# Storing the outputs of a mixture of experts: 8 KB runs for experts 0 to 5, own buffers and transfers for experts 6 and 7, three semaphores by turns on one DMA queue

## The chip, the cores and the metric

The kernel runs on one core of one Trainium2 chip. The metric is device time in microseconds (us) of one execution. A profile of one execution gives a span, from the first to the last instruction, and what each engine did in it. The engines are PE (TensorE, matmuls), DVE (VectorE), ACT (ScalarE), POOL (GpSimd) and SP (SyncE). Transfers between device memory (HBM) and the on-chip memory (SBUF) are carried out by 16 DMA engines. A transfer is issued by an engine's queue: here most come from Pool's queue (the profile calls it software_dynamic), two from SyncE's (hardware_dynamic). Each transfer counts a semaphore up by 16 when its data has landed.

## The reference

Eight experts, each a two-layer network with a ReLU between, over 256 tokens of width 512. Data is fp32 outside; the kernel computes in bf16 with fp32 sums.

```python
n_experts, capacity, hidden, expert_hidden = 8, 256, 512, 2048
# x [8, 256, 512], w1 [8, 512, 2048], w2 [8, 2048, 512], all float32

def reference(x, w1, w2):
    h = np.matmul(x, w1)
    h = np.maximum(h, 0)
    return np.matmul(h, w2).astype(np.float32)   # [8, 256, 512]
```

Each expert has 4 MB of w1 and 4 MB of w2 in fp32, so 64 MB of weights are read in all. x and the output are 4 MB each.

## The kernel before

P is 128 (partitions), E, C, H, F are 8, 256, 512, 2048, and MC = C/P = 2. R = E\*C/P = 16 is the number of rows of x in one partition. The views say which row of a DRAM tensor goes to which partition. In the output's view, partition p of an expert holds rows 2p and 2p+1, that is 4 KB in a row in DRAM:

```python
    x_v = x.rearrange("e (pp r) k -> (e pp) (r k)", r=R)
    w1_v = w1.rearrange("e (p ko) n -> p e (ko n)", ko=K1)
    w2_v = w2.rearrange("e (p h j) n -> p e h (j n)", h=2, j=JH)
    out_v = out.rearrange("e (p mo) k -> p e (mo k)", mo=MC)
    # ...
    out_sb = allot("out_sb", [P, E, MC, H], FP32)
```

Weights are converted to bf16 on the way in, by Pool's queue, into four slots each for w1 and w2. The order of the loads, and a semaphore for each slot:

```python
    d_w = {
        (w, i): sem(f"d_w{w}_{i}")
        for w, slots in [(1, (0, 2, 3)), (2, (0, 1, 2, 3))]
        for i in slots
    }
    d_half, d_pool, d_last = sem("d_half"), sem("d_pool"), sem("d_last")
    # ...
    loads = []                                   # (which weight, experts, half, halves)
    for es in [(0, 1), (2, 3)]:
        loads += [(1, es, 0, 2), (2, es, 0, 2)]
    loads += [(1, (4, 5), 0, 2), (2, (4,), 0, 2), (2, (5,), 0, 2)]
    for e in range(6, E - 1):
        loads += [(1, (e,), 0, 2), (2, (e,), 0, 2)]
    loads += [(1, (E - 1,), 0, 2), (2, (E - 1,), 0, 1), (2, (E - 1,), 1, 1)]
```

SyncE loads the first quarter of x (`x_head`), tells TensorE of every load that has landed, and at the end stores the last expert's output:

```python
        sp = nc.sync
        for i, (w, es, h, n) in enumerate(loads):
            sp.wait_ge(*landed[i])
            sp.sem_inc((c_w1, c_w2)[w - 1], n * len(es) if w == 2 else len(es))
        sp.wait_ge(v_last, MC)
        sp.dma_start(
            out_v[:, E - 1, :], out_sb[:, E - 1].rearrange("p m h -> p (m h)")
        ).then_inc(d_last, 16)
```

Pool issues the rest of x, then the loads (each waits only until its slot is free), one tiny store of 16 x 16 values between the two halves of the last w2, and, once that tiny store has landed, one store of the outputs of experts 0 to 6:

```python
        pool = nc.gpsimd
        pool.dma_start(x_sb[:, HEAD * H:], x_v[:, HEAD * H:]).then_inc(d_pool, 16)
        # ... identity ...
        for i, (w, es, h, n) in enumerate(loads):
            old = es[-1] - NS
            if w == 2 and 2 in es:
                tc.wait_critical_data_deps()
                pool.wait_ge(*after_transposes(K1 * MC))
            if old >= 0 and h == 0:
                if w == 1:
                    pool.wait_ge(*after_hidden(old, NG))
                else:
                    pool.wait_ge(*after_outputs(old, MC))
            if i == len(loads) - 1:
                pool.wait_ge(s_event, 3)
                pool.dma_start(
                    out_v[:16, 0, :16], out_sb[:16, 0, 0, :16]
                ).then_inc(d_pool, 16)
            # ... src, dst of the load ...
            pool.dma_start(dst, src).then_inc(landed[i][0], 16)
        pool.wait_ge(s_event, 4)
        pool.wait_ge(d_pool, 32)
        pool.dma_start(
            out_v[:, :E - 1, :], out_sb[:, :E - 1].rearrange("p e m h -> p e (m h)")
        ).then_inc(d_pool, 16)
```

x is transposed by TensorE through PSUM (`xt_ps`); DVE and ACT copy it into `xT`, in the order of rows in which the outputs then come out. DVE takes the outputs out of PSUM (`o_ps`, two banks of 128 x 512), but for the last half, which ACT takes:

```python
        def copy_xt(copy, ko, m):
            return copy(
                xT[:, ko, m].rearrange("k (ep r2) -> k ep r2", r2=R // MC),
                xt_ps[m][:].rearrange("k r2 ep -> k ep r2"),
            )
        # ...
        for e in range(E):
            for m in range(MC):
                if e == E - 1 and m == 1:
                    break
                dve.wait_ge(*after_outputs(e, m + 1))
                cp = dve.tensor_copy(out_sb[:, e, m, :], o_ps[m][:])
                cp.then_inc(v_last if e == E - 1 else c_o)
            if e in (4, E - 2):
                dve.drain().then_inc(s_event)
        # ... on ACT, after the last expert's last matmul:
        act.copy(out_sb[:, E - 1, 1, :], o_ps[1][:]).then_inc(v_last)
```

TensorE takes each expert in two halves of the hidden layer and then the output layer (16 pairs of matmuls into the two banks). At the end of each half it takes one count of `c_o`, which stands for a bank of outputs that has been copied out:

```python
        def half():
            # ... 32 matmuls into h_ps ...
                if ends:
                    take(c_h, 1)
                    if i == n - 1:
                        take(c_o, MC // 2)
        def expert():
            take(c_w1, 1)
            loop("half", reg["half"], 2, half)
            for k in range(K2):
                if k % JH == 0:
                    take(c_w2, 1)
                # ... 2 matmuls into o_ps, the last pair counts s_pe ...
```

Of the kernel before, what the change touches and what calls it, by code (L numbers as in the profile page):

```python
# [8 lines left out]
FP32 = mybir.dt.float32  # L9
# [7 lines left out]
def kernel(  # L17
# [8 lines left out]
    P = 128  # L26
    E, C, H = x.shape
    F = w1.shape[2]
    MC = C // P
# [3 lines left out]
    R = E * C // P  # L33

    HEAD = 4

    NS = 4
# [8 lines left out]

    x_v = x.rearrange("e (pp r) k -> (e pp) (r k)", r=R)
    w1_v = w1.rearrange("e (p ko) n -> p e (ko n)", ko=K1)  # L50
    w2_v = w2.rearrange("e (p h j) n -> p e h (j n)", h=2, j=JH)
    out_v = out.rearrange("e (p mo) k -> p e (mo k)", mo=MC)


    places, free = {}, FIRST_FREE
# [1 line left out]
    def allot(name, shape, dtype):  # L57
        nonlocal free
        places[name] = free
        t = nc.alloc_sbuf_tensor_at(name, shape, dtype, offset=free)  # L60
        free += math.prod(shape[1:]) * mybir.dt.size(dtype)
        return t


    out_sb = allot("out_sb", [P, E, MC, H], FP32)
    w1_sb = allot("w1_sb", [P, NS, K1 * F], BF16)
    w2_sb = allot("w2_sb", [P, NS, K2 * H], BF16)
    xT = allot("xT", [P, K1, MC, E * P], BF16)
# [4 lines left out]
    x_sb = w2_sb[:, 2, :]  # L73
    X_AT = W2_AT + 2 * K2 * H * 2

    xt_ps = [nc.alloc_psum_tensor(f"xt_ps{i}", [P, R // MC, P], BF16) for i in range(MC)]
    h_ps = [nc.alloc_psum_tensor(f"h_ps{i}", [P, GJ * C], FP32) for i in range(UG)]
    o_ps = [nc.alloc_psum_tensor(f"o_ps{i}", [P, H], FP32) for i in range(MC)]

    def sem(name):  # L80
        return tc.alloc_semaphore(name)

    d_w = {
        (w, i): sem(f"d_w{w}_{i}")
        for w, slots in [(1, (0, 2, 3)), (2, (0, 1, 2, 3))]
        for i in slots
    }
    d_half, d_pool, d_last = sem("d_half"), sem("d_pool"), sem("d_last")  # L90


    s_event = sem("s_event")
    s_pe, v_last = sem("s_pe"), sem("v_last")

    def after_transposes(n):
        return s_pe, n

    def after_hidden(e, groups):
        return s_pe, K1 * MC + e * (NG + MC) + groups  # L100

    def after_outputs(e, halves):
        return s_pe, K1 * MC + e * (NG + MC) + NG + halves
# [10 lines left out]
    loads = []  # L114
# [3 lines left out]
    for e in range(6, E - 1):  # L118
        loads += [(1, (e,), 0, 2), (2, (e,), 0, 2)]
    loads += [(1, (E - 1,), 0, 2), (2, (E - 1,), 0, 1), (2, (E - 1,), 1, 1)]  # L120
    landed, counts = [], {}
    for w, es, h, _ in loads:
        s = d_half if h else d_w[w, es[0] % NS]
        counts[id(s)] = counts.get(id(s), 0) + 16
        landed.append((s, counts[id(s)]))

# [4 lines left out]
    with tc.tile_critical(no_gpsimd_drain=True):  # L133

        sp = nc.sync
        for i, (w, es, h, n) in enumerate(loads):
            sp.wait_ge(*landed[i])
            sp.sem_inc((c_w1, c_w2)[w - 1], n * len(es) if w == 2 else len(es))
        sp.wait_ge(v_last, MC)
        sp.dma_start(  # L140
            out_v[:, E - 1, :], out_sb[:, E - 1].rearrange("p m h -> p (m h)")
        ).then_inc(d_last, 16)


        pool = nc.gpsimd
        pool.dma_start(x_sb[:, HEAD * H:], x_v[:, HEAD * H:]).then_inc(d_pool, 16)  # L146
        pool.memset(identity[:], 0.0).then_inc(s_event)  # L147
        pool.wait_ge(s_event, 1)

# [1 line left out]
            out=identity[:],  # L151
# [7 lines left out]
# [13 lines that stand above are left out]


                pool.wait_ge(s_event, 3)
                pool.dma_start(  # L175
                    out_v[:16, 0, :16], out_sb[:16, 0, 0, :16]
                ).then_inc(d_pool, 16)
            e, ne, at_slot = es[0], len(es), es[0] % NS
            if w == 2:
                src = w2_v[:, e:e + ne, h:h + n, :].rearrange("p e h n -> p e (h n)")  # L180
                dst = w2_sb[:, at_slot:at_slot + ne, h * JH * H:(h + n) * JH * H]
            else:
                src, dst = w1_v[:, e:e + ne, :], w1_sb[:, at_slot:at_slot + ne, :]
            pool.dma_start(dst, src).then_inc(landed[i][0], 16)  # L184
        pool.wait_ge(s_event, 4)
        pool.wait_ge(d_pool, 32)
        pool.dma_start(  # L187
            out_v[:, :E - 1, :], out_sb[:, :E - 1].rearrange("p e m h -> p e (m h)")
        ).then_inc(d_pool, 16)

        def copy_xt(copy, ko, m):
            return copy(  # L194
                xT[:, ko, m].rearrange("k (ep r2) -> k ep r2", r2=R // MC),
                xt_ps[m][:].rearrange("k r2 ep -> k ep r2"),
            )


        dve = nc.vector  # L200
        dve.sem_inc(c_xt[0], 1)
        for ko in range(K1):
            dve.wait_ge(*after_transposes(ko * MC + 1))
            copy_xt(dve.tensor_copy, ko, 0).then_inc(c_xt[0])
        dve.sem_inc(c_o, MC)
        for e in range(E):
            for m in range(MC):
                if e == E - 1 and m == 1:
                    break
                dve.wait_ge(*after_outputs(e, m + 1))  # L210
                cp = dve.tensor_copy(out_sb[:, e, m, :], o_ps[m][:])  # L211
                cp.then_inc(v_last if e == E - 1 else c_o)
            if e in (4, E - 2):
                dve.drain().then_inc(s_event)  # L214


        act = nc.scalar
        act.sem_inc(c_xt[1], 1)
        for ko in range(K1):
            act.wait_ge(*after_transposes(ko * MC + 2))  # L220
            copy_xt(act.copy, ko, 1).then_inc(c_xt[1])
# [6 lines left out]
                    mybir.ActivationFunctionType.Relu,  # L228
                ).then_inc(c_h)
        act.wait_ge(*after_outputs(E - 1, MC))  # L230
        act.copy(out_sb[:, E - 1, 1, :], o_ps[1][:]).then_inc(v_last)  # L231

# [1 line left out]
        pe = nc.tensor  # L236
# [45 lines left out]
        def last_column(step):  # L282

            return (P - 1) * step * 2
# [25 lines left out]
                t.then_inc(s_pe)  # L310

        pe.wait_ge(s_event, 2)
        pe.wait_ge(d_pool, 16)
        x_first = X_AT + last_column(K1)
        pe.reg_mov(reg["x"], x_first)
        loop("transposes", reg["x"], x_first + K1 * 2, transposes)
# [116 lines left out]


        pool.drain()
        pool.wait_ge(d_pool, 48).then_inc(s_event)
        pool.wait_ge(d_last, 16).then_inc(s_event)


# [28 lines left out]
```

## Time and profile before

| | |
|---|---|
| device time, median of 3 runs | 180.59 us (180.55 to 180.62) |
| span of the profiled execution | 178.7 us |
| TensorE busy | 127.7 us, 71% of the span |
| DVE busy | 15.8 us, 9% |
| ACT busy | 38.7 us, 22% |
| POOL busy | 10.2 us, 6% |
| HBM read and written | 71.30 MB and 4.20 MB |
| one eviction, DVE, 128 x 512 fp32 | 687 ns |
| one copy of transposed x, DVE and ACT, 128 x 1024 | 1225 ns and 1012 ns |

The page cuts the span into 40 equal slices (4.47 us each) and gives for each the busy share in tenths; the row "DMA" is the mean busy share of the 16 DMA engines, "GB/s" what they moved. A weight load reads fp32 and writes bf16, and GB/s counts it about once, by what lands. Further parts list the DMA queues with their packets, the chain of work that ended last, and for each transfer the time from issue to landing. L264 is the line of the helper that records every matmul, L138 is SyncE's wait for a load, L211 and L231 are the evictions on DVE and ACT.

### The profile page before, as it was taken

To read this page: it belongs to the slowest core of one execution; us is meant where nothing else is said; L and a number is where in the kernel's file an instruction comes from. 1 tells how busy PE (TensorE), PEld (TensorE's weight loads), DVE (VectorE), ACT (ScalarE), POOL (GpSimd) and SP (SyncE) were. 2 spreads that over 40 slices of the span, in tenths; PEclk is the share of its full clock that TensorE was granted. 3 is DMA by queue.
4 is the path that set the end of the run, shared out by engine and by line. 5 is a ranking of instruction groups with operands and counts; after the bars stand their busy time and mean duration, and the time that the engine had idled before them with its cause. 6 is when DMAs were issued, how large, how long until landed. Compare 5 with 4: busy or idle time off the path is not lost. (4 is left out here: it accounts for less than half of the span.)

```text
span 178.7 us, 2096 instructions
## 1 busy us (share of the span) xinstructions
PE 127.7 (71%) x832; PEld 89.8 (50%) x832; DVE 15.8 (9%) x20; ACT 38.7 (22%) x38; POOL 10.2 (6%) x21
## 2 busy tenths in 40 slices
PE   0008610792049999993079999999999999769990
PEld 0006600691014695693024984884794695359630
DVE  0204320000000200200000200200200200200010
ACT  0202420062000062044000260251152062004400
POOL 6100010000000002101000110100200000002000
PEclk9999999999657999999759999999999999978999
DMA  6999998998999999999899899999999989989996
GB/s 211 244 220 205 235 227 183 235 231 183 231 235 205 205 235 209 202 235 231 180 235 231 191 224 235 205 205 235 209 202 235 231 180 235 231 182 220 327 424 259
DMA packets 3744, 40.37 MB, mean 226 GB/s; under 512 B 288, under 2 KB 288, under 8 KB 1312
## 3 DMA queue, kind: packets, MB, share of 16 engines
q0 software_dynamic: 3456, 38.80, 97.3%
q1 hardware_dynamic: 288, 1.57, 2.4%
HBM read 71.30 MB, written 4.20 MB: 422 GB/s over the span
## 5 line engine op out<-in xcount | busy, mean ns | idle before, releaser
L264 PE MATMUL o_ps<-w_sb,hT 128*128 x256 | 60.3, 396 | 18.9 <-PEq L239 18.8
L264 PE MATMUL h_ps<-xT,w_sb 128*128 x512 | 61.4, 282 | 11.8 <-PEq L239 11.8
L264 PEld LDWEIGHTS h_ps<-xT,w_sb 128*128 x512 | 58.0, 146 | 16.1 <-issue 12.5
L225 ACT ACTIVATE hT<-h_ps 128x1024 bf16<-128x1024 f32 x32 | 32.7, 1023 | 111.2 <-PE h_ps L264 111.2
L264 PEld LDWEIGHTS o_ps<-w_sb,hT 128*128 128x128 bf16 x256 | 25.3, 101 | 51.2 <-issue 24.6
L211 DVE COPY out_sb<-o_ps 128x512 f32<-128x512 f32 x15 | 9.7, 687 | 141.2 <-PE o_ps L264 141.2
L264 PE MATMUL xt_ps<-identity,w_sb 128*128 128x128 bf16 x64 | 7.6, 312 | 15.5 <-PEq L239 15.5
L264 PEld LDWEIGHTS xt_ps<-identity,w_sb 128*128 x64 | 6.5, 147 | 16.3 <-issue 16.3
L184 POOL DMA_DIRECT2D w_sb<-in_w_dram x12 | 7.4, 618 | 104.3 <-PE h_ps L264 57.3
L194 ACT COPY xT<-xt_ps 128x1024 bf16<-128x1024 bf16 x4 | 4.0, 1012 | 11.8 <-PE xt_ps L264 11.8
L194 DVE COPY xT<-xt_ps 128x1024 bf16<-128x1024 bf16 x4 | 4.9, 1225 | 11.8 <-PE xt_ps L264 11.8
L187 POOL DMA_DIRECT2D out_dram<-out_sb x1 | 1.0, 962 | 34.0 <-DMA out_dram<-out_sb 34.0
L194 ACT ACT_TABLE_LOAD x1 | 1.3, 1283 | 7.0 <-DVE w_sb L132 7.0
L231 ACT COPY out_sb<-o_ps 128x512 f32<-128x512 f32 x1 | 0.6, 585 | 5.9 <-PE o_ps L264 5.9
L132 DVE CAST w_sb<-x_head 128x2048 bf16<-128x2048 f32 x1 | 1.2, 1227 | 5.5 <-DMA x_head<-in_x_dram 5.5
L175 POOL DMA_DIRECT2D out_dram<-out_sb x1 | 0.5, 509 | 14.7 <-DVEq L214 14.7
L146 POOL DMA_DIRECT2D w_sb<-in_x_dram x1 | 0.7, 679 | 0.8 <-POOLq L452 0.8
L150 POOL TENSOR_SCALAR_AFFINE_SELECT identity<-identity 128x128 bf16<-128x128 bf16 x1 | 0.3, 283 | 0.2 <-POOL identity L147 0.2
L147 POOL MEMSET identity<- 128x128 bf16 x1 | 0.2, 223 | 0.0
L452 POOL MEMSET const-float32-0.0<- 128x1 f32 x1 | 0.1, 93 | 0.2 <-issue 0.2
L452 POOL MEMSET const-bfloat16-1.0<- 128x1 bf16 x1 | 0.1, 95 | 0.0
L452 POOL MEMSET const-uint8-127<- 128x1 uint8 x1 | 0.1, 95 | 0.0
(1 smaller groups left out, 0.1 us busy)
## 6 DMA issues: line engine op xcount, KB each, us to landing
w_sb<-in_w_dram POOLq DMA_DIRECT2D x5, 4096.0 KB, 47.9
w_sb<-in_w_dram POOLq DMA_DIRECT2D x5, 2048.0 KB, 51.5
out_dram<-out_sb POOLq DMA_DIRECT2D x1, 3584.0 KB, 12.9
w_sb<-in_w_dram POOLq DMA_DIRECT2D x2, 1024.0 KB, 44.1
w_sb<-in_x_dram POOLq DMA_DIRECT2D x1, 1536.0 KB, 11.5
x_head<-in_x_dram SPq DMA_DIRECT2D x1, 1024.0 KB, 4.7
out_dram<-out_sb SPq DMA_DIRECT2D x1, 512.0 KB, 3.1
out_dram<-out_sb POOLq DMA_DIRECT2D x1, 1.0 KB, 34.4
```

Source lines behind the costliest of these rows:

```text
L132: nc.vector.tensor_copy(x_sb[:, :HEAD * H], x_head[:])
L146: pool.dma_start(x_sb[:, HEAD * H:], x_v[:, HEAD * H:]).then_inc(d_pool, 16)
L150: pool.affine_select(out=identity[:], in_=identity[:], compare_op=mybir.AluOpType.not_equal, fill=1.0, base=0, pattern=[[-1, P]], channel_ ...
L175: pool.dma_start(out_v[:16, 0, :16], out_sb[:16, 0, 0, :16]).then_inc(d_pool, 16)
L184: pool.dma_start(dst, src).then_inc(landed[i][0], 16)
L187: pool.dma_start(out_v[:, :E - 1, :], out_sb[:, :E - 1].rearrange("p e m h -> p e (m h)")).then_inc(d_pool, 16)
L194: return copy(xT[:, ko, m].rearrange("k (ep r2) -> k ep r2", r2=R // MC), xt_ps[m][:].rearrange("k r2 ep -> k ep r2"),)
L211: cp = dve.tensor_copy(out_sb[:, e, m, :], o_ps[m][:])
L225: act.activation(hT[:, g * GJ:(g + 1) * GJ, :].rearrange("p a c -> p (a c)"), h_ps[g % UG][:], mybir.ActivationFunctionType.Relu,).then_in ...
L231: act.copy(out_sb[:, E - 1, 1, :], o_ps[1][:]).then_inc(v_last)
L264: return pe.add_instruction(inst)
L452: nc = _bacc.Bacc("TRN2", target_bir_lowering=False, num_devices=1)
```

## The change

The outputs of experts 0 to 5 are gathered in pairs of experts. Expert 2i lies on partitions 0 to 63 and expert 2i+1 on partitions 64 to 127, four rows to a partition, so that what one partition holds of an expert is 8 KB in a row in DRAM instead of 4 KB. Experts 6 and 7 get a buffer `last_sb` with two rows to a partition on all 128 partitions; there partition 64t + q holds rows 4q + 2t and 4q + 2t + 1. The order of rows in which PSUM receives the outputs is changed to suit, by the copies of x. The store of experts 0 to 6 becomes two: one of experts 0 to 5, one of expert 6. All Pool transfers count three semaphores by turns, and each waits for the one three before it in place of having semaphores by slot. The aim is longer runs in the stores and fewer semaphores.

```diff
-    out_v = out.rearrange("e (p mo) k -> p e (mo k)", mo=MC)
+    HP = P // 2
+    PAIRS = E // 2 - 1
+    out_pairs = out[:2 * PAIRS].rearrange("(i s) (q r) k -> s q i (r k)", s=2, r=2 * MC)
+    out_v = out.rearrange("e (q t m) k -> t q e (m k)", t=2, m=MC)
@@
-    out_sb = allot("out_sb", [P, E, MC, H], FP32)
+    out_sb = allot("out_sb", [P, PAIRS, 2 * MC, H], FP32)
+    last_sb = allot("last_sb", [P, 2, MC, H], FP32)
@@ (the semaphores by slot)
-    d_w = { ... }
-    d_half, d_pool, d_last = sem("d_half"), sem("d_pool"), sem("d_last")
+    d_pool, d_last = [sem(f"d_pool{i}") for i in range(3)], sem("d_last")
@@
+    of_load = [i + 1 for i in range(len(loads) - 1)] + [len(loads) + 1]
+    small, bulk, bulk2 = len(loads), len(loads) + 2, len(loads) + 3
+
+    def landed(i):
+        return d_pool[i % 3], 16 * (i // 3 + 1)
@@ (SyncE)
-            sp.wait_ge(*landed[i])
+            sp.wait_ge(*landed(of_load[i]))
...
         sp.dma_start(
-            out_v[:, E - 1, :], out_sb[:, E - 1].rearrange("p m h -> p (m h)")
+            out_v[:, :, E - 1, :], last_sb[:, 1].rearrange("p m h -> p (m h)")
         ).then_inc(d_last, 16)
@@ (Pool; all its transfers go through queue)
+        def queue(i, dst, src):
+            if i >= 3:
+                pool.wait_ge(*landed(i - 3))
+            pool.dma_start(dst, src).then_inc(d_pool[i % 3], 16)
+
+        queue(0, x_sb[:, HEAD * H:], x_v[:, HEAD * H:])
...
+                queue(small, out_pairs[0, :16, 0, :16], out_sb[:16, 0, 0, :16])
...
+            queue(of_load[i], dst, src)
+        pool.wait_ge(*landed(small))
         pool.wait_ge(s_event, 4)
-        pool.wait_ge(d_pool, 32)
-        pool.dma_start(
-            out_v[:, :E - 1, :], out_sb[:, :E - 1].rearrange("p e m h -> p e (m h)")
-        ).then_inc(d_pool, 16)
+        queue(bulk, out_pairs, out_sb[:].rearrange("p i r h -> p i (r h)"))
+        pool.wait_ge(s_event, 5)
+        queue(bulk2, out_v[:, :, E - 2, :], last_sb[:, 0].rearrange("p m h -> p (m h)"))
@@ (the copies)
         def copy_xt(copy, ko, m):
-            return copy(
-                xT[:, ko, m].rearrange("k (ep r2) -> k ep r2", r2=R // MC),
-                xt_ps[m][:].rearrange("k r2 ep -> k ep r2"),
-            )
+            for t in range(2):
+                inst = copy(
+                    xT[:, ko, m].rearrange(
+                        "k (e t pp r4) -> k t e pp r4", e=E, t=2, r4=R // 4
+                    )[:, t],
+                    xt_ps[m][:].rearrange(
+                        "k (r4 t) (e pp) -> k t e pp r4", t=2, e=E
+                    )[:, t],
+                )
+            return inst
+
+        def copy_out(copy, e, m):
+            if e >= 2 * PAIRS:
+                return copy(last_sb[:, e - 2 * PAIRS, m, :], o_ps[m][:])
+            i, s = divmod(e, 2)
+            for t in range(2):
+                inst = copy(
+                    out_sb[s * HP:(s + 1) * HP, i, t * MC + m, :],
+                    o_ps[m][t * HP:(t + 1) * HP, :],
+                )
+            return inst
@@ (DVE; ACT's last copy likewise goes through copy_out)
-                cp = dve.tensor_copy(out_sb[:, e, m, :], o_ps[m][:])
+                cp = copy_out(dve.tensor_copy, e, m)
...
-            if e in (4, E - 2):
+            if e in (0, E - 3, E - 2):
                 dve.drain().then_inc(s_event)
```

The loads, the matmuls and TensorE's waits are as before, apart from the names of the semaphores.

More of the change, by code (lines that the diff above doesn't have):

```diff
@@ L81, in sem @@
         return tc.alloc_semaphore(name)
[L85 to L89, printed above, removed]
-    d_half, d_pool, d_last = sem("d_half"), sem("d_pool"), sem("d_last")
+    d_pool, d_last = [sem(f"d_pool{i}") for i in range(3)], sem("d_last")
     s_event = sem("s_event")
@@ L120 @@
     loads += [(1, (E - 1,), 0, 2), (2, (E - 1,), 0, 1), (2, (E - 1,), 1, 1)]
[L121 to L125, printed above, removed]
+    of_load = [i + 1 for i in range(len(loads) - 1)] + [len(loads) + 1]
+    small, bulk, bulk2 = len(loads), len(loads) + 2, len(loads) + 3
+    def landed(i):
+        return d_pool[i % 3], 16 * (i // 3 + 1)
     x_pool = ctx.enter_context(tc.tile_pool(name="x_pool", bufs=1))
@@ L140 @@
         sp.dma_start(
-            out_v[:, E - 1, :], out_sb[:, E - 1].rearrange("p m h -> p (m h)")
+            out_v[:, :, E - 1, :], last_sb[:, 1].rearrange("p m h -> p (m h)")
         ).then_inc(d_last, 16)
         pool = nc.gpsimd
-        pool.dma_start(x_sb[:, HEAD * H:], x_v[:, HEAD * H:]).then_inc(d_pool, 16)
+        def queue(i, dst, src):
[3 more added lines that the diff above has]
+        queue(0, x_sb[:, HEAD * H:], x_v[:, HEAD * H:])
         pool.memset(identity[:], 0.0).then_inc(s_event)
@@ L174 @@
                 pool.wait_ge(s_event, 3)
-                pool.dma_start(
-                    out_v[:16, 0, :16], out_sb[:16, 0, 0, :16]
-                ).then_inc(d_pool, 16)
+                queue(small, out_pairs[0, :16, 0, :16], out_sb[:16, 0, 0, :16])
             e, ne, at_slot = es[0], len(es), es[0] % NS
@@ L183 @@
                 src, dst = w1_v[:, e:e + ne, :], w1_sb[:, at_slot:at_slot + ne, :]
-            pool.dma_start(dst, src).then_inc(landed[i][0], 16)
+            queue(of_load[i], dst, src)
+        pool.wait_ge(*landed(small))
         pool.wait_ge(s_event, 4)
-        pool.wait_ge(d_pool, 32)
-        pool.dma_start(
-            out_v[:, :E - 1, :], out_sb[:, :E - 1].rearrange("p e m h -> p e (m h)")
-        ).then_inc(d_pool, 16)
+        queue(bulk, out_pairs, out_sb[:].rearrange("p i r h -> p i (r h)"))
+        pool.wait_ge(s_event, 5)
+        queue(bulk2, out_v[:, :, E - 2, :], last_sb[:, 0].rearrange("p m h -> p (m h)"))
         def copy_xt(copy, ko, m):
-            return copy(
-                xT[:, ko, m].rearrange("k (ep r2) -> k ep r2", r2=R // MC),
-                xt_ps[m][:].rearrange("k r2 ep -> k ep r2"),
-            )
+            for t in range(2):
[18 more added lines that the diff above has]
+            return inst
         dve = nc.vector
@@ L230 @@
         act.wait_ge(*after_outputs(E - 1, MC))
-        act.copy(out_sb[:, E - 1, 1, :], o_ps[1][:]).then_inc(v_last)
+        copy_out(act.copy, E - 1, 1).then_inc(v_last)
         pe = nc.tensor
@@ L312 @@
         pe.wait_ge(s_event, 2)
-        pe.wait_ge(d_pool, 16)
+        pe.wait_ge(*landed(0))
         x_first = X_AT + last_column(K1)
@@ L435 @@
         pool.drain()
-        pool.wait_ge(d_pool, 48).then_inc(s_event)
+        for i in (bulk, bulk2):
+            pool.wait_ge(*landed(i)).then_inc(s_event)
         pool.wait_ge(d_last, 16).then_inc(s_event)
```

## The prediction

> **What bounds the kernel now.** First I read the slices of the span on the page: what is busy all the time, and where that stops.
>
> ```profile
> PE   0008610792049999993079999999999999769990
> ...
> DMA  6999998998999999999899899999999989989996
> GB/s 211 244 220 205 235 227 183 235 231 183 231 235 205 205 235 209 202 235 231 180 235 231 191 224 235 205 205 235 209 202 235 231 180 235 231 182 220 327 424 259
> DMA packets 3744, 40.37 MB, mean 226 GB/s; under 512 B 288, under 2 KB 288, under 8 KB 1312
> ...
> q0 software_dynamic: 3456, 38.80, 97.3%
> q1 hardware_dynamic: 288, 1.57, 2.4%
> ```
>
> The 16 DMA engines are full from end to end; TensorE has holes. For some 167 us the stream is weights (about 215 GB/s of bf16 landing, from twice as many bytes of fp32 read), and then, in the last two and a half slices, stores. Next, the chain that ended last, in order of time, and SyncE's waits for the weights:
>
> ```profile
> 158.08 8.85 PE h_ps L264 x64
> 166.93 6.97 PE o_ps L264 x32
> ...
> 173.92 0.58 ACT out_sb L231
> ...
> SPq L138 <- DMA w_sb<-in_w_dram: 160.6, 12, 25.3
> ```
>
> SyncE's twelve waits, asked for by window, end at 32.1 us and then 19.3 us apart for each pair and 9.7 us for each single expert; the last two, for the halves of the last w2, end 4.9 us apart, at 167.7. So w1 of expert 7 is there at about 157.8, and the end of the kernel hangs on that: 16 us of matmuls, an eviction, one store. What lands then is in the DMA issues and in one-microsecond windows of the tail (columns: length; busy time of PE, weight loads, DVE, ACT, POOL; clock; DMA share; GB/s):
>
> ```profile
> out_dram<-out_sb POOLq DMA_DIRECT2D x1, 3584.0 KB, 12.9
> ...
> out_dram<-out_sb SPq DMA_DIRECT2D x1, 512.0 KB, 3.1
> ...
> 166.00:167.00 1.00, 1.00 (x10) 0.82 (x9) 0.00 (x0) 0.28 (x2) 0.00 (x0) 1.00 0.75 160
> 167.00:168.00 1.00, 1.00 (x6) 0.48 (x5) 0.00 (x0) 0.99 (x1) 0.00 (x0) 1.00 0.99 397
> ...
> 171.00:172.00 1.00, 1.00 (x7) 0.41 (x6) 0.00 (x0) 0.00 (x0) 0.00 (x0) 1.00 1.01 418
> ...
> 176.00:177.00 1.00, 0.00 (x0) 0.00 (x0) 0.00 (x0) 0.00 (x0) 0.00 (x0) 1.00 1.00 410
> 177.00:178.00 1.00, 0.00 (x0) 0.00 (x0) 0.00 (x0) 0.00 (x0) 0.00 (x0) 1.00 0.06 21
> ```
>
> The stores begin in the slice from 166 to 167 (I take 166.7) and run at about 418 GB/s, which is 26.1 GB/s for each of 16 engines. The timeline has Pool's store issued at 163.57, so it is down at 176.5, and SyncE's at 174.53, down at 177.6. The last byte moves at about 177.05; 0.6 us later the landing is seen, and 1.1 us later the span ends. Device time is 1.9 us over the span (180.59 against 178.7).
>
> Two packet counts say how the stores were spread. The hardware queue's 288 packets are two transfers of 128 rows, each with 16 small ones that count the semaphore: 2 x (128 + 16). Both transfers used all 16 engines.
>
> [...]
>
> **The change part by part.**
>
> *Bulk store, experts 0 to 5.* Rows of 8 KB in place of 4 KB, 384 in place of 896 (seven experts). The program's DRAM pattern is 128 x 3 x 2048: the two experts of a pair and the 64 row groups of each merge, because 64 groups of 2048 elements are just one expert. [...] 3.15 MB at 418 GB/s are 7.5 us: 166.7 to 174.2. The longer rows could help only if 4 KB rows ran below the engines' limit, but with 4 KB rows the engines already show a share of 1.01 busy. Gain: none that I would count.
>
> *Expert 6, now a transfer of its own, and expert 7.* This is where I expect the cost. Their buffer holds rows in a new order (row 4q + 2t + m at partition 64t + q), so the DRAM side is t, q, (m k): the built program carries 2 x 64 x 1024. The step of t (1024 elements) is below that of q (2048), so these two don't merge. SBUF's side has 128 partitions. [...] Each of two engines then moves 64 rows of 4 KB, 262 KB, where before each of 16 moved 33 KB. At 26.1 GB/s that is 10.0 us in place of 1.25.
>
> Expert 7's store is the last thing on the path. Issue stays at 174.5. From issue to first byte I estimate 1.3 us: the same queue's x_head, 1 MB, took 4.7 us, of which 2.5 are 65.5 KB per engine at 26.1 GB/s and 0.6 the landing's report; that leaves 1.6, some of it shared with the second load of x. Then 174.5 + 1.3 + 10.0 + 0.6 = 186.4 for the landing, in place of 177.6; plus 1.1 is a span of 187.5, plus 1.9 a device time of 189.4. The engines of the bulk are free at 174.2, before the first byte of this store.
>
> Expert 6's store goes out on Pool's queue right behind the bulk: 174.2 + 10.0 + 0.6 = 184.8 if it has its two engines for itself. That is below 186.4, so it isn't the end, unless both stores got the same pair (below).
>
> *Three semaphores by turns.* Each Pool transfer waits for the one three before it. With landings at 12.7 (x), 32.1, 51.4, 70.7, 90.0, 109.3, 119.0, 128.7, 138.4, 148.0, 157.7 and 162.6, w1 of experts 2 and 3 goes out at 12.7 instead of 5, w2 of experts 2 and 3 at 32.1 instead of 23.4, w1 of expert 6 at 109.3 instead of 82.3, and so on. Two transfers are still queued at each such moment, and the shortest stock is at the end: the second half of the last w2 goes out at 157.7, with 4.9 us of the first half ahead. An issue costs 0.5 to 0.75 us, and the first transfers on this queue moved data within about 2 us of issue. So the stream has no gap: 0 us. The tiny marker store is issued at 148.0 in place of 128.5, but lands where it did (162.9), and the bulk still goes out at about 163.5.
>
> *Copies of x.* Eight copies of 1225 ns on DVE and 1012 ns on ACT (four on each) become sixteen of half the elements. With the durations of 512 elements (687 and 585 ns), a pair costs 1.37 on DVE and 1.17 on ACT: 0.15 us more for each, four times, 0.6 us. The transposes end near 23 us and TensorE waits for weights until 32.2: hidden.
>
> *Copies of the outputs.* For experts 0 to 5 each eviction becomes two of 64 partitions, each as long as one of 128. Per expert 4 x 0.65 = 2.6 us on DVE instead of 1.3. TensorE needs the first bank back at the end of half of the next hidden layer, 3.6 us later, the second after 7.2; it gets them after 1.3 and 2.6. Hidden. Experts 6 and 7 have one copy per half as before.
>
> Sum: 8.8 us on the last store, 0 elsewhere: 180.6 + 8.8 = 189.4.
>
> **The rivals.** *Both small stores on the same pair of engines.* [...] 20 us of packets lie on these two engines from 174.2 on, and by alternation both end near 174.2 + 20.0 + 0.6 = 194.8; with 1.1 and 1.9 that is 197.8. For it: every other transfer of this program takes all 16 engines[...] I give it 0.27.
>
> *All 16 engines after all*, because something between program and engines splits or merges the pattern. Then the same bytes end at the same 177.05 as now, with one more transfer behind: 180.5 to 181.5. [...] I give it 0.05.
>
> *The Pool waits bite:* if a semaphore reached Pool late, the DMA engines would stand still a microsecond or two before w1 of expert 7, and all that follows shifts. The margins above speak against it. It would come on top: 190 to 192.
>
> *A faster or slower single engine.* The 26.1 GB/s are from 16 engines at once. Two alone might go at a somewhat different rate; 10% is 1 us.
>
> **Range and chances.** 0.65 for about 189.4 with 1.5 us either way, 0.27 for about 198, the rest for little change or for more than I see. I predict 189.4; the range must hold both: 187.3 to 198.8. Slower by over 2% (above 184.2): 0.94. Within 2%: 0.05. Faster: 0.01.
>
> **What would show it.** The hardware queue's packets fall from 288 to 274 (128 + 16 and 128 + 2). SyncE's store takes about 12 us to land in place of 3.1; Pool's store of 512 KB about 20 from its issue near 164.5. In the windows, after about 174.5, the moved bytes drop from 418 to 52 GB/s while one small store is on its way and to about 105 with both on different pairs; a steady 52 to the end would be the collision. SyncE's waits still end at the same times up to 167.7 and matmuls of expert 7 still start at 158.1. It would be wrong if the last store landed in 3 us, or if matmuls started later.

## The result, and the profile after

The changed kernel takes 198.33 us (197.84 to 198.97, 6 runs) against 180.56 us before: 1.0989 times as long, 95% interval 1.0967 to 1.1011. That is 17.8 us more. I had put the number at 189.4, so the direction was right and the size half of what came; the rival with both small stores on the same two engines said 197.8.

The page of the changed kernel, in slices of 4.93 us (a span of 197.2 us in 40), and its queues:

```profile
PE   0036504940599999406999999999999699900000
...
DMA  7999999999999999999999999999999899951110
GB/s 240 212 233 216 216 213 213 213 213 213 213 213 229 226 223 219 216 216 213 213 213 213 213 213 213 219 233 223 223 213 216 189 213 226 429 196 48 53 52 33
DMA packets 4258, 40.38 MB, mean 205 GB/s; under 512 B 1186, under 2 KB 1186, under 8 KB 1442
...
q0 software_dynamic: 3984, 38.80, 88.5%
q1 hardware_dynamic: 274, 1.57, 2.1%
```

Up to slice 35 it runs like the kernel before. Then come four slices at about 50 GB/s that weren't there, in which no engine computes: two DMA engines of sixteen, at 26 GB/s each. The hardware queue's 274 packets are 128 + 16 for x_head and 128 + 2 for the last store, so that store used two engines. The chain and the issues show that nothing ahead of the stores is later:

```profile
158.15 7.31 PE h_ps L289 x64
165.46 6.97 PE o_ps L289 x32
...
172.45 0.58 ACT last_sb L215
...
out_dram<-out_sb POOLq DMA_DIRECT2D x1, 3072.0 KB, 11.9
...
out_dram<-last_sb POOLq DMA_DIRECT2D x1, 512.0 KB, 29.1
out_dram<-last_sb SPq DMA_DIRECT2D x1, 512.0 KB
```

Matmuls of expert 7 start at 158.15 (158.08 before). Expert 6's store is issued at 164.24 by the timeline and lands 29.1 us later, at 193.3. For SyncE's store the page has no landing, where the page of the kernel before has one, of 3.1 us. The windows of the tail, with the columns as before (the last is GB/s):

```profile
173.00:174.00 1.00, 0.00 (x0) 0.00 (x0) 0.00 (x0) 0.03 (x1) 0.00 (x0) 1.00 0.97 410
174.00:175.00 1.00, 0.00 (x0) 0.00 (x0) 0.00 (x0) 0.00 (x0) 0.00 (x0) 1.00 0.96 240
175.00:176.00 1.00, 0.00 (x0) 0.00 (x0) 0.00 (x0) 0.00 (x0) 0.00 (x0) 1.00 0.27 46
...
180.00:181.00 1.00, 0.00 (x0) 0.00 (x0) 0.00 (x0) 0.00 (x0) 0.00 (x0) 0.50 0.13 53
...
194.00:195.00 1.00, 0.00 (x0) 0.00 (x0) 0.00 (x0) 0.00 (x0) 0.00 (x0) 0.50 0.12 49
195.00:196.00 1.00, 0.00 (x0) 0.00 (x0) 0.00 (x0) 0.00 (x0) 0.00 (x0) 0.50 0.05 20
```

A DMA share of 0.13 is that of two full engines of sixteen (0.125). It stays there from 176 to 195, through the whole of both stores. Had each store had a pair of its own, the share would be 0.25 while both run (0.26 is measured in the next run). Twenty microseconds of two engines are 1 MB: both small stores, on the same two.

The trace's single packets, counted by queue, show the sharing itself. From 179 to 192 us SyncE's queue starts 6 to 8 rows of 4 KB in each microsecond, and Pool's as many. Pool's last row ends at 192.90; in the next two microseconds SyncE's queue starts 14 and 12. So each store had half of the two engines while both ran. The first row of expert 7 moves only at 177.94, though its store is issued at 173.06.

### The profile page after: what moved, and what is told of

Same layout as the page of the kernel before. It is cut to its first block, busy times and chain, and to the rows that moved or that the text cites. A ratio compares the mean times of both kernels' runs of the same rounds, so it can differ in the third digit from the quotient of the medians.

```text
span 197.2 us, 2129 instructions
## 1 busy us (share of the span) xinstructions
PE 126.8 (64%) x832; PEld 89.4 (45%) x832; DVE 24.9 (13%) x36; ACT 38.9 (20%) x42; POOL 10.9 (6%) x22
## 3 DMA queue, kind: packets, MB, share of 16 engines
q0 software_dynamic: 3984, 38.80, 88.5%
## 5 line engine op out<-in xcount | busy, mean ns | idle before, releaser
L289 PE MATMUL h_ps<-xT,w_sb 128*128 x512 | 60.6, 280 | 11.0 <-PEq L264 11.0
L218 DVE COPY out_sb<-o_ps 64x512 f32<-64x512 f32 x24 | 16.5, 689 | 104.4 <-PE o_ps L289 104.1
L154 POOL DMA_DIRECT2D w_sb<-in_w_dram x12 | 7.3, 613 | 139.0 <-DMA w_sb<-in_w_dram 86.8
L203 DVE COPY xT<-xt_ps 128x512 bf16<-128x512 bf16 x8 | 5.2, 686 | 11.8 <-PE xt_ps L289 11.8
L203 ACT COPY xT<-xt_ps 128x512 bf16<-128x512 bf16 x8 | 4.3, 588 | 11.8 <-PE xt_ps L289 11.8
L215 DVE COPY last_sb<-o_ps 128x512 f32<-128x512 f32 x3 | 2.0, 689 | 26.2 <-PE o_ps L289 26.2
L215 ACT COPY last_sb<-o_ps 128x512 f32<-128x512 f32 x1 | 0.6, 585 | 5.9 <-PE o_ps L289 5.9
L154 POOL DMA_DIRECT2D out_dram<-last_sb x1 | 0.9, 868 | 0.0
## 6 DMA issues: line engine op xcount, KB each, us to landing
out_dram<-last_sb POOLq DMA_DIRECT2D x1, 512.0 KB, 29.1
```

The lines of the kernel that those rows point to most:

```text
L154: pool.dma_start(dst, src).then_inc(d_pool[i % 3], 16)
L203: inst = copy(xT[:, ko, m].rearrange("k (e t pp r4) -> k t e pp r4", e=E, t=2, r4=R // 4)[:, t], xt_ps[m][:].rearrange("k (r4 t) (e pp) -> ...
L215: return copy(last_sb[:, e - 2 * PAIRS, m, :], o_ps[m][:])
L218: inst = copy(out_sb[s * HP:(s + 1) * HP, i, t * MC + m, :], o_ps[m][t * HP:(t + 1) * HP, :],)
L289: return pe.add_instruction(inst)
```

## The experiments

My theory after the result, A: the two stores of 512 KB take two engines each, and which two a store of Pool gets depends on what Pool's transfers before it took in the same execution, so that they meet on the same two in every run. Rivals: B, a two-engine transfer gets the same two engines whatever was issued before it; C, what earlier executions took counts as well; or the waits by turns, the doubled copies or the row order cost the time.

**Another marker store.** The tiny marker store, ahead of everything that matters, becomes a two-engine transfer too.

```diff
-                queue(small, out_pairs[0, :16, 0, :16], out_sb[:16, 0, 0, :16])
+                queue(
+                    small,
+                    out_pairs[0, :16, 0, :16].rearrange("(a b) k -> b a k", b=2),
+                    out_sb[:16, 0, 0, :16],
+                )
```

(It writes its 16 x 16 values to other rows; the bulk store writes over them in both cases.)

> Same two stores on two engines each as in the changed kernel, but the tiny marker store, earlier on Pool's queue, is now also a two-engine transfer (2 x 8 rows against 16 partitions). Theory A [...]: [...] the collision is gone: 188 to 189.5 us, and in the tail about 105 GB/s while both stores run. Theory B [...]: unchanged, 198.3 us and 53 GB/s. Theory C [...]: single runs scatter between about 188.5 and 198.

Measured: 190.34 us (189.83 to 190.77, 4 runs). Another pattern in a transfer of 1 KB takes 8.0 us off the kernel. Its tail:

```profile
175.00:176.00 1.00, 0.00 (x0) 0.00 (x0) 0.00 (x0) 0.00 (x0) 0.00 (x0) 1.00 0.33 62
...
182.00:183.00 1.00, 0.00 (x0) 0.00 (x0) 0.00 (x0) 0.00 (x0) 0.00 (x0) 0.50 0.26 106
...
186.00:187.00 1.00, 0.00 (x0) 0.00 (x0) 0.00 (x0) 0.00 (x0) 0.00 (x0) 0.50 0.13 53
```

Four engines (0.26) at 106 GB/s while both stores run, two at 53 when one is left. That fits theory A; theory B falls. The spread of 0.9 us in four runs, and of 1.1 us in the six of the changed kernel, has none of the 8 us jumps of theory C. The median is 0.8 us above the range I had given for A: from 176 to 180 us the four engines move only 61 to 94 GB/s, a slow start that comes back in the runs below.

**Two marker stores on eight engines each.** The marker of the changed kernel is 16 packets of 64 B, as in the kernel before. If the engines that Pool's transfers take add up, 8 + 8 count as that marker did, and the stores meet again; if it is enough that some transfer before them takes fewer than sixteen, they stay apart.

```diff
-                queue(small, out_pairs[0, :16, 0, :16], out_sb[:16, 0, 0, :16])
+                queue(
+                    small,
+                    out_pairs[0, :16, 0, :16].rearrange("(a b) k -> b a k", b=8),
+                    out_sb[:16, 0, 0, :16],
+                )
+                pool.dma_start(
+                    out_pairs[0, 16:32, 0, :16].rearrange("(a b) k -> b a k", b=8),
+                    out_sb[16:32, 0, 0, :16],
+                ).then_inc(d_extra, 16)
@@
         pool.wait_ge(*landed(small))
+        pool.wait_ge(d_extra, 16)
```

> The changed kernel with two marker stores on Pool's queue, each of 8 x 2 rows of 16 values, so on eight engines each. [...] the collision is there again: 198 us and 53 GB/s to the end. [...] if any transfer of fewer than 16 engines before it breaks the meeting, 190.3 us.

Measured: 198.77 us (198.41 to 199.38, 4 runs), with 49 to 57 GB/s from 182 us to 196:

```profile
185.00:186.00 1.00, 0.00 (x0) 0.00 (x0) 0.00 (x0) 0.00 (x0) 0.00 (x0) 0.50 0.13 53
...
190.00:191.00 1.00, 0.00 (x0) 0.00 (x0) 0.00 (x0) 0.00 (x0) 0.00 (x0) 0.50 0.12 49
```

The meeting is back. So it isn't enough that earlier transfers take fewer than sixteen engines: with a marker on two the stores are apart (190.34), with 8 + 8 they meet (198.77) as with the plain one of 16 packets (198.33). The number of transfers doesn't decide either: it is the same with the plain marker and with that on two engines, and one more with 8 + 8. These three cases fit engines that add up from transfer to transfer, and come back to the same place at sixteen; other sums were not run. All ten runs of this kernel and the changed one lie between 197.84 and 199.38 us, so in each Pool's store took the pair of SyncE's. What sets the place at the start, and which two engines these are, the runs don't show. (The profiled run of this version has its loads 1.3 us later from the first on; the end, set by two full engines, hardly moves.)

**Expert 7's store on sixteen engines.** Two transfers of 64 partitions, each with 64 as its slowest dimension on both sides.

```diff
-        sp.dma_start(
-            out_v[:, :, E - 1, :], last_sb[:, 1].rearrange("p m h -> p (m h)")
-        ).then_inc(d_last, 16)
+        for t in range(2):
+            sp.dma_start(
+                out_v[t, :, E - 1, :],
+                last_sb[t * HP:(t + 1) * HP, 1].rearrange("p m h -> p (m h)"),
+            ).then_inc(d_last[t], 16)
```

> Expert 7's store as two transfers of 64 partitions x 4 KB, each on 16 engines; expert 6's store stays on two engines. Theory A and B: nothing shares the two engines for long, and the end is set by expert 6 alone: data from about 174.5 to 184.6, landing 185.2, plus 1.1 to the end of the span, plus 1.9: 188.2 us. A theory that the new order of rows or the waits by turns cost the time, and not the number of engines, gives 197 to 198.

Measured: 190.74 us (190.27 to 190.97, 4 runs). That is far from the 197 to 198 of a cost in the order of rows or the waits, so neither of these is the cause; but it is 2.5 us over the 188.2 that I had worked out. Part of that I had left out: expert 7's halves now pass through expert 6's two engines as well (524 KB / 16 = 33 KB each, 1.25 us at 26.1 GB/s). Expert 6's store landed at 164.33 + 22.5 = 186.8, 1.6 us after my 185.2; the span ended 2.1 us after that landing where I had taken 1.1.

**Expert 6's store on sixteen engines**, expert 7's left on two: the sum of my prediction by itself.

```diff
-        queue(bulk2, out_v[:, :, E - 2, :], last_sb[:, 0].rearrange("p m h -> p (m h)"))
+        for t in range(2):
+            queue(
+                bulk2 + t,
+                out_v[t, :, E - 2, :],
+                last_sb[t * HP:(t + 1) * HP, 0].rearrange("p m h -> p (m h)"),
+            )
```

> Expert 6's store as two transfers of 64 partitions on 16 engines each; expert 7's store stays on two engines. This is the sum of my prediction by itself: issue at 173.1 to 174.5, 1.3 us to the first byte, 10.0 us of data on two engines, 0.6 to the landing, 1.1 and 1.9: 188.0 to 189.4 us. If a lone engine is faster or slower than its share of 26 GB/s in a full stream, it shows here: 10% is 1 us.

Measured: 190.26 us (189.97 to 190.43, 4 runs), 0.9 over the upper end of my sum (189.4). Where that is, the windows of its tail show:

```profile
176.00:177.00 1.00, 0.00 (x0) 0.00 (x0) 0.00 (x0) 0.00 (x0) 0.00 (x0) 0.66 0.15 49
177.00:178.00 1.00, 0.00 (x0) 0.00 (x0) 0.00 (x0) 0.00 (x0) 0.00 (x0) 0.50 0.13 33
178.00:179.00 1.00, 0.00 (x0) 0.00 (x0) 0.00 (x0) 0.00 (x0) 0.00 (x0) 0.50 0.12 33
179.00:180.00 1.00, 0.00 (x0) 0.00 (x0) 0.00 (x0) 0.00 (x0) 0.00 (x0) 0.50 0.13 49
180.00:181.00 1.00, 0.00 (x0) 0.00 (x0) 0.00 (x0) 0.00 (x0) 0.00 (x0) 0.50 0.13 53
```

Both engines count as busy from 176 (0.13 and more), but move 164 KB in four microseconds where 53 GB/s would be 212 KB: 48 KB short, which are 0.9 us.

**Both on sixteen engines** (both edits above). What is left of the change is all that I had taken for free.

> Both stores as two transfers of 64 partitions on 16 engines each. All that is left of the change is the 8 KB rows, the waits by turns, the doubled copies and one or two transfers more. My theory (those are worth nothing): 180.3 to 181.5 us. If 64 partitions of one half give only half the rate, 1 MB takes 2.5 us longer and this is 182 to 183. If the waits by turns cost something, matmuls of expert 7 start later than 158.1.

Measured: 181.13 us (180.69 to 181.43, 11 runs), 1.0025 times the kernel before, interval 1.0013 to 1.0037. So 17.2 of the 17.8 us go with the number of engines of the two stores.

**Where the last half microsecond is.** First without the waits by turns, by giving each Pool transfer a semaphore of its own:

```diff
-    d_pool, ... = [sem(f"d_pool{i}") for i in range(3)], ...
+    d_pool, ... = [sem(f"d_pool{i}") for i in range(17)], ...
-        return d_pool[i % 3], 16 * (i // 3 + 1)
+        return d_pool[i], 16
-            if i >= 3:
-                pool.wait_ge(*landed(i - 3))
-            pool.dma_start(dst, src).then_inc(d_pool[i % 3], 16)
+            pool.dma_start(dst, src).then_inc(d_pool[i], 16)
```

> The version with both small stores on 16 engines, but with a semaphore of its own for each Pool transfer and no waits by turns; that version took 181.13 us, 0.55 over the kernel before, and its loads landed 0.2 to 0.3 us later from the middle on. If the waits by turns cost that, this gives 180.6 to 180.8 us. If the remaining half microsecond is the longer tail of four small stores, it stays at 181.0 to 181.3.

Measured: 181.09 us (180.68 to 181.68, 13 runs), ratio 1.0029 (1.0018 to 1.0041). No difference: the waits by turns cost nothing that shows. Then two parts of the repair, each alone in the kernel before. The last store in halves:

```diff
-        sp.dma_start(
-            out_v[:, E - 1, :], out_sb[:, E - 1].rearrange("p m h -> p (m h)")
-        ).then_inc(d_last, 16)
+        for t in range(2):
+            part = slice(t * 64, (t + 1) * 64)
+            sp.dma_start(
+                out_v[part, E - 1, :], out_sb[part, E - 1].rearrange("p m h -> p (m h)")
+            ).then_inc(d_last[t], 16)
```

> The kernel before with the last store as two transfers of 64 partitions, on 16 engines each, rows in the right order. The version of the changed kernel with both small stores on 16 engines is 0.5 us slower than the kernel before, with or without the waits by turns. If that is the second issue and the half-partition transfers at the end, it shows here: 180.9 to 181.2 us. If not, 180.5 to 180.7.

Measured: 181.06 us (180.50 to 181.80, 13 runs), ratio 1.0025 (1.0013 to 1.0037). And expert 6 as a transfer of its own, on 128 partitions:

```diff
-            out_v[:, :E - 1, :], out_sb[:, :E - 1].rearrange("p e m h -> p e (m h)")
+            out_v[:, :E - 2, :], out_sb[:, :E - 2].rearrange("p e m h -> p e (m h)")
         ).then_inc(d_pool, 16)
+        pool.dma_start(
+            out_v[:, E - 2, :], out_sb[:, E - 2].rearrange("p m h -> p (m h)")
+        ).then_inc(d_six, 16)
```

> The kernel before with the store of experts 0 to 6 cut in two: 0 to 5, and expert 6 by itself on 128 partitions and 16 engines. If one more transfer behind the bulk costs the half microsecond: 180.9 to 181.2 us. If not, 180.5 to 180.7.

Measured: 180.57 us (180.47 to 181.24, 14 runs), ratio 1.0003 (0.9994 to 1.0012). So one more transfer on Pool's queue is free, and the last store in two issues costs 0.5 us: as much as the version with both stores repaired is slower. I take it that the half microsecond comes with my repair; whether by the second issue or by the halves is not separated. The rest of the change is then neither gain nor loss within what these runs resolve.

**The two engines alone, without the rest of the change.** In the kernel before, the last store writes its rows in another order (expert 7's output rows come out permuted), so that its pattern doesn't merge:

```diff
+    last_v = out[E - 1].rearrange("(q t m) k -> t q (m k)", t=2, m=MC)     # 8 and 16 in the next two
@@
-            out_v[:, E - 1, :], out_sb[:, E - 1].rearrange("p m h -> p (m h)")
+            last_v, out_sb[:, E - 1].rearrange("p m h -> p (m h)")
```

> The kernel before with one change: the last expert's store writes its rows to DRAM in another order, as 2 x 64 x 1024 (so the rows of expert 7 come out permuted), which puts it on two engines. Nothing else of the change is in it, and the store of experts 0 to 6 stays one transfer on 16 engines, so there is no collision. If the number of engines is the whole cause: 190.0 to 190.6 us (10 us of data, plus about 0.9 us of slow start, as in the version that left only expert 7 on two engines, 190.26). If the rest of the change had a part in that loss, it is less, down to 185.

Measured: 189.71 us (189.40 to 191.39, 4 runs), ratio 1.053 (1.0486 to 1.0574). One pattern in one store of 512 KB costs 9.1 us. Its median is 0.3 below the range I had given. The issue in its one profile is earlier (173.12, against 174.49 in the version with only expert 7 on two engines), but the first row moves at 175.79 against 175.89, so that is not the reason; the last row ends 0.55 earlier, at 186.57 against 187.12, after a shorter slow start.

With t = 8:

> As the kernel before with the permuted last store, but as 8 x 16 x 1024, so on eight engines with 65.5 KB each. The bulk of experts 0 to 6 leaves the engines at about 175.5; then 2.5 us, 0.6 to the landing, 1.1 and 1.9: 181.6 us, 1.0 over the kernel before. If any split other than 16 had a fixed penalty, it is 183 or more.

Measured: 183.41 us (182.48 to 183.68, 4 runs), ratio 1.0144 (1.0118 to 1.017). The hardware queue's packets are 280, which is 128 + 16 + 128 + 8: eight engines, as expected. But the loss is 2.8 us, not 1.0. With t = 16:

> As the two kernels before with a permuted last store, but as 16 x 8 x 1024: slowest dimensions 16 and 128, so sixteen engines with 32.8 KB each, as in the kernel before; only the form of the pattern and the order of rows differ. The eight-engine form took 183.41 us where 181.6 was expected, with the moved bytes at 86 to 152 GB/s where eight engines at 26 GB/s would move 210. If the loss beyond the byte count is in the form or the order of rows, it is here too: 181.5 to 182.5 us. If it comes with engines that are alone, it is gone: 180.5 to 180.8.

Measured: 181.25 us (181.16 to 181.37, 5 runs), ratio 1.0038 (1.0025 to 1.0051), between what the two readings gave. The windows of the two at the end, first with t = 8, then with t = 16:

```profile
176.00:177.00 1.00, 0.00 (x0) 0.00 (x0) 0.00 (x0) 0.00 (x0) 0.00 (x0) 0.61 0.65 107
177.00:178.00 1.00, 0.00 (x0) 0.00 (x0) 0.00 (x0) 0.00 (x0) 0.00 (x0) 0.50 0.37 86
178.00:179.00 1.00, 0.00 (x0) 0.00 (x0) 0.00 (x0) 0.00 (x0) 0.00 (x0) 0.50 0.45 152
179.00:180.00 1.00, 0.00 (x0) 0.00 (x0) 0.00 (x0) 0.00 (x0) 0.00 (x0) 0.50 0.39 152
```

```profile
176.00:177.00 1.00, 0.00 (x0) 0.00 (x0) 0.00 (x0) 0.00 (x0) 0.00 (x0) 0.57 1.09 217
177.00:178.00 1.00, 0.00 (x0) 0.00 (x0) 0.00 (x0) 0.00 (x0) 0.00 (x0) 0.50 0.75 287
```

Eight engines stay under the 210 GB/s of their share throughout, sixteen start at 217 where the kernel before had 410 in the same microsecond. So the form or the order of rows costs 0.7 us even at sixteen engines. At eight engines the excess over the byte count is 1.8 us (183.41 against 181.6, which is the "183 or more" that I had named for a fixed penalty of any split other than 16). At two it is 0.9 or less (190.26 against 189.4), so the excess does not simply grow as the engines get fewer.

A slow start is common to these stores at 2, 8 and 16 engines. In the kernel before each of the first 24 rows of the last store takes 159 ns on its engine; with t = 16 it is 280 to 322 ns for 16 of 24. The cause is open, but two candidates lose weight. One is the longer issue (0.63 us by the timeline for t = 16, where the plain store has 0.35): with t = 2 the issue is over at 173.76 and the first row moves at 175.79, yet the rate is 33 GB/s from 177 to 178. The other is the order of rows with t = 2, which is that of the changed kernel. With both small stores on sixteen engines, expert 7 is stored in that same order, by two plain patterns, and the tail has no slow start:

```profile
175.00:176.00 1.00, 0.00 (x0) 0.00 (x0) 0.00 (x0) 0.00 (x0) 0.00 (x0) 0.50 1.01 406
176.00:177.00 1.00, 0.00 (x0) 0.00 (x0) 0.00 (x0) 0.00 (x0) 0.00 (x0) 0.50 1.03 418
```

That leaves the pattern of three dimensions, and for t = 16 an order in which neighbouring partitions lie 32 rows apart in place of 4. I haven't tried these apart.

## Why the prediction was wrong in size

*The step that failed* is the choice of the branch, in "The rivals": both small stores on the same pair got 0.27, and the number 189.4 stood on the other branch. In the six runs of the changed kernel, and in four with markers of 8 + 8, the stores met every time; with the marker on two engines, never in four. I had no run that showed which two engines a store of Pool gets, and weighed as chance, by an estimate of my own, what came out the same in every run. The collision is 198.33 - 190.34 = 8.0 us. In one thing the rival was off as well: it had both stores end together near 194.8, but expert 7's rows began to take their turn only at 177.94, so expert 6 ended at 192.90 and expert 7 at 195.85.

*The number of engines of the two stores* was right: 274 packets, a share of 0.13, 53 GB/s. No trace of the kernel before showed a store on fewer than sixteen engines; that these would take two was my assumption, and it is the runs that show it. *Its size* was short by 0.9 us: 10.0 us of data became 11.2 (first row at 175.89, end of the last at 187.12) by a slow start, and 0.9 of that shows in the time (190.26 in place of 189.4). Together: 9.1 for two engines (190.26 - 181.13), 8.1 for the meeting (198.33 - 190.26), 0.55 for the rest, which sum to the 17.8.

*The bulk store.* No gain from 8 KB rows: right as far as seen. The store of 3 MB ran at 410 to 467 GB/s from 168 to 174, where 4 KB rows had 401 to 434 in the same microseconds; no time was shorter for it.

*The waits by turns*: right, nothing (181.09 without, 181.13 with). Pool now waits for DMA for 86.8 us in all ahead of loads, and the loads' landings stay within half a microsecond (the last at 168.1, before 167.7). A long wait of the issuer, with two transfers still queued, was no loss here.

*The copies of x and of the outputs*: hidden, as said. DVE takes 2.81 us per expert for four copies of 64 x 512, 689 ns each, where 128 x 512 took 687 ns; its busy time rose from 15.8 to 24.9 us and TensorE started expert 7 where it did.

*The issue of the last store* I had left at 174.5; it was at 173.06 in the profiled run. The reason is in the last section. It makes no difference to the end, and the 1.3 us that I took from issue to first byte did not set the start. With expert 6 by itself in the kernel before, the last store is issued at 173.04 and its first row moves at 175.61; in the kernel before it is issued at 174.53, and the first row moves at 175.65. In both, Pool's last row starts at 175.9.

## What to carry to other kernels

Before a store is reordered, look at the slowest dimension of both sides of its pattern as the program carries it, not at how many partitions the tile has. Here 2 x 64 rows against 128 partitions went to two of sixteen engines (274 packets, a share of 0.13), 8 x 16 rows to eight (280 packets), and 16 x 8 rows, halves of 64 rows and 128 rows filled all sixteen (shares of 1.09, 1.03 and 1.00 from 176 to 177 us); with two, a 512 KB store on the end of the path grew by 9 us. With 16 in that dimension the kernel lost 0.7 us, with the store cut into two pieces of 64 rows 0.5 us. Where two transfers on few engines can't be avoided, one by SyncE and one by Pool, reckon with their meeting on the same engines in every run, as these did in ten of ten: read the DMA share in the tail, 2/16 or 4/16, to see whether they did, and change what Pool's earlier transfers take, which here, with a marker of 1 KB, was worth 8.0 us.

## What I had not expected

*Packets of 4 bytes beside a two-engine store, on the software queue.* A two-engine store of 128 rows by Pool adds 896 packets of 4 bytes: the changed kernel has 3984 on that queue, the version with expert 6 cut in two for sixteen engines 3104. Rows are 128 in both, and two transfers have 16 more counts than one (the kernel before has 240 packets of 4 bytes on this queue for 15 transfers); 3984 - (3104 - 16) = 896 = 14 x 64, as many as fourteen engines with one small packet for each of the 64 rows that a busy engine moves. The trace names no engine for a packet, so that is a reading of the counts. The two-engine marker fits it: two packets of 512 B, which are eight rows of 64 B each, and fourteen of 32 B, eight times 4. The issue takes 868 ns in place of 551 for a plain one of 128 rows (in the kernel before with expert 6 by itself). On SyncE's queue there are none: its 18 small packets are the 16 + 2 above.

*Whether TensorE's clock dips goes with a tenth of a microsecond of waiting.* In twelve profiles of this study TensorE waits between 1.5 and 2.8 us for w1 of expert 7. In the seven with up to 2.24 us the 64 matmuls take 7.31 or 7.32 us, in the other five, and in the kernel before (2.62 us), from 2.37 us on, 8.85 us, with a granted clock that falls to 0.5 in the windows of those matmuls. The two forms in the timeline, first with expert 6 by itself, then the kernel before (the wait stands in brackets):

```profile
158.12 7.31 PE L267 MATMUL h_ps<-xT,w_sb 128*128 x64 [1.53 <-PEq L242]
158.08 8.85 PE L264 MATMUL h_ps<-xT,w_sb 128*128 x64 [2.62 <-PEq L239]
```

The line between 2.24 and 2.37 is what these profiles show and no rule. In the traces of both kernels the clock changes at times that lie 3.41 us or a multiple of it apart (before 35.50, 45.74, 55.98, 86.70, 93.53, 158.38, 161.79; changed 44.11, 54.35, 85.07, 95.31, 177.23), so where a wait falls between such times may matter beside its length; no run separates the two. The last store is issued 1.4 us earlier or later for it. In the kernel before this has no weight, as its stores stream until 177 us in any case: with expert 6's store by itself the last one is issued at 173.04 in place of 174.53, and the time is the same (180.57).
